# Outputs of 28 heads as float32r products, gains in chunk 0's rows, decays behind the keys, two more chunks of squares on VectorE

## The chip, the core and the metric

The kernel runs on one core of a Trainium2 chip. The core has a matrix engine (TensorE, PE in the profile; its weight loads are PEld), a vector engine (VectorE, DVE), a scalar engine (ScalarE, ACT), GpSimd (POOL), a sync engine that issues most transfers (SyncE, SP), and 16 DMA engines. The engines run their own instruction lists in order and wait for one another by semaphores. The metric is the device time of one execution in microseconds, as the median of several runs.

## The reference

The program is a two-layer decoder trunk on 256 tokens with 16 learned prefix tokens in front (T = 272), width 2048, 16 heads of 128, everything in float32.

```python
h = concat(meta_tokens, x)                       # 272 x 2048
for layer in (0, 1):
    a = rms_norm(h, norm_attn[layer])
    if layer == 0:                               # forgetting attention
        q, k, v, f = split(a @ fox_w_in)
        c = cumsum(log_sigmoid(f + fox_b_f))
        s = q k^T * scale + c[q] - c[k], masked; p = softmax(s); o = p v
        h = h + o @ fox_w_o
    else:                                        # stick-breaking attention, shared K and V
        k, v = split(rms_norm(h, kv_norm) @ w_kv); q = a @ sb_w_q
        z = q k^T * scale
        p = exp(log_sigmoid(z) + later sums of log_sigmoid(-z)), masked; o = p v
        h = h + o @ sb_w_o
    h = h + relu(rms_norm(h, norm_mlp[layer]) @ w_up) ** 2 @ w_down
return rms_norm(h, final_norm)[16:]
```

Queries are handled in blocks: the 16 prefix tokens, then two blocks of 128. A block sees the keys up to its own end.

## The kernel before

Activations lie feature-major: 16 chunks of 128 features on the partitions, tokens along the free axis. `hT` is the residual stream. A weight matrix is streamed in 128x1024 pieces `raw` (two k-chunks of 512 columns) on SP's queue through four buffers.

**Products in three parts.** Large products are not made in float32. A float32 operand is split into a part hi, rounded to float32r, and the remainder lo: ACT copies hi, DVE subtracts lo. For weights these are `whi` and `wlo` (L220, L221), each with a ring of four buffers; for activations the object `Split` holds them (`x_a`, `x_o`, `x_u` and others). `gemm_group` (products at L168) computes four chunks of output, in the accumulators `acc_0` to `acc_3`, over 16 k-chunks in four blocks `kb`, with three float32r products for each pair of k-chunk and output chunk: hi with hi, hi with lo, lo with hi. Small products, in attention and norms, are made in float32 directly; the profile draws such a product as two records (x2).

**Attention.** Heads come in four groups of four. For each group of layer 0 one `gemm_group` makes the queries, one the keys and one the values; layer 1 makes all queries first and then keys and values by group. Scores are put into a tile `s`, one of three buffers with the tag "s". In layer 0 `decays` (L483) first fills `s` with forget-gate differences and mask, from `fk`, which arrives by a transfer. `evac_k` writes the keys `kT` (L337) and their hi and lo parts `kh` and `kl` (L339). The probabilities are turned key-major by 32x32 transposes and copies, `turned` into `pt`, and the values token-major by `token_major` into `vt` (L380). Both are cut into pieces that `PLANS` puts at the `kb` steps of the next `gemm_group`, behind the splits of that step's weights; `turns` makes this table.

`outputs` (L415 to L447) then makes the four heads' outputs: a small product `pc` for corner parts, and for each head one float32 product `po` of 128x256 (L421: the first key block for both query blocks) and one of 128x128 (L424: the second key block for the second query block). DVE adds the corner parts (L426), and `put_split` writes the outputs as hi and lo (L446 on ACT, L447 on DVE) into `x_o`. Outputs of one group run at the end of the next group's query product in layer 0, and before block 3 of its key product in layer 1; those of the last group of each layer run inside the first group of the output projection, `out_proj`.

**Start.** `load_x` loads `hT` in chunks (L261) between the pieces of the first weight (L203), with the six norm gains `g_sb` as a transfer of their own behind chunk 0 (L263). `split_chunk` scales and splits a chunk (ACT L122, DVE L123).

**End.** The final norm needs the sum of squares over the 16 chunks of the last residual. Chunks 0 to 11 are squared on ACT and summed on DVE (`normf.add`, L140). `add_squares` (L676) multiplies this sum, and the squares of chunks 12, 13 and 14 each, with a column of 1/2048 on PE, two products of 128x1 each time; chunk 15 follows at L703. Three products `warm` (L718) follow, then `pr_fin` (L723), which spreads the factor, and the output is scaled on DVE and GpSimd and stored.

**What sets the order.** The kernel is written in a tile framework that orders instructions by a simulated timeline at build time. `tc.issue_after` and `behind` (an order without a semaphore, on PE) fix single places, and `pinned` keeps the products of a `gemm_group` in written order. So the written order is only a part of the actual order, which is shown below where it matters.

Of the kernel before, what the change touches and what calls it, by code (L numbers as in the profile page):

```python
# [34 lines left out]
def yoco_kernel(ctx: ExitStack, tc: tile.TileContext, hT_in, gains, b_f, w_f, w_qkv0, w_o0, w_up, w_dn,  # L35
# [17 lines left out]
    hT = const.tile([P, NC, T], F32, name="hT")  # L53
    g_sb = const.tile([P, 6, NC], F32, name="g_sb")
# [124 lines left out]
    def gemm_group(wblk, sp, t0, evac, before={}, after={}, load_x=None, widen=False, mid={}):  # L179
# [9 lines left out]
        for kb in range(4):  # L189
# [15 lines left out]
            for hf in range(2):  # L205
# [11 lines left out]
                for o, no, c0, c1 in boxes:  # L217
                    src = raws[hf][:, o:o + no, c0:c1]
# [40 lines left out]
    def load_x(chunks):  # L259
        c0, n = chunks[0], len(chunks)  # L260
        nc.sync.dma_start(hT[:, c0:c0 + n, :], hT_in[:, c0:c0 + n, :])  # L261
        if c0 == 0:
            nc.sync.dma_start(g_sb, gains)  # L263
        for c in chunks:
            split_chunk(xa, G_A0, c)
# [65 lines left out]
    def keys(label):  # L331
# [4 lines left out]
        def evac(m, acc):  # L336
            nc.vector.tensor_tensor(out=kT[:, m, :], in0=acc, in1=box["rstd"], op=ALU.mult)  # L337
            nc.scalar.activation(kh[:, m, :], kT[:, m, :], AF.Copy)
            nc.vector.tensor_tensor(out=kl[:, m, :], in0=kT[:, m, :], in1=kh[:, m, :].bitcast(F32), op=ALU.subtract)  # L339
# [11 lines left out]
    def turned(s, label):  # L351
# [13 lines left out]
        return pt.rearrange("p (h k) -> p h k", h=4), piece  # L365
# [6 lines left out]
    def token_major(vT, label):  # L372
# [9 lines left out]
        return vt.rearrange("p h (b t) -> p h b t", t=P), piece  # L382
# [5 lines left out]
    def turns(turn_p, turn_v, p, v):  # L388
# [23 lines left out]
    def outputs(g, ao, p, v, pm_sb, vm_sb, label):  # L412
# [4 lines left out]
        for pr in range(2):  # L417
            po = patt.tile([P, 2, 256], F32, tag="patt", name=f"po_{label}_{pr}")
            for i in range(2):
                j = 2 * pr + i  # L420
                ins = nc.tensor.matmul(po[:, i, :], v[:, j, 0, :], p[:, j, :2 * P], start=i == 0, stop=False)  # L421
                if i == 0:
                    behind(ins)
                nc.tensor.matmul(po[:, i, P:], v[:, j, 1, :], p[:, j, 2 * P:], start=False, stop=i == 1)  # L424
# [26 lines left out]
    for g in range(4):  # L451
# [28 lines left out]
        def decays(j):  # L480

            for i, (o, n) in enumerate(((0, 144), (144, T))):
                nc.vector.scalar_tensor_tensor(out=s[:, j, o:o + n], in0=fk[:, j, :n],  # L483
                                               scalar=fq_sb[:, i, 4 * g + j:4 * g + j + 1],
                                               in1=maskA[:, o:o + n], op0=ALU.subtract, op1=ALU.add)
# [22 lines left out]
        def meta(g=g, qm=qm, kT=kT, s0=s0, fk=fk):  # L508
# [3 lines left out]
            nc.vector.scalar_tensor_tensor(out=s0.rearrange("p (h k) -> p h k", h=4), in0=fk[:, :, :32],  # L512
                                           scalar=fqm_sb[:, g:g + 1], in1=maskM, op0=ALU.subtract, op1=ALU.add)
# [7 lines left out]
        probs, turn_p = turned(s, f"0_{g}")  # L521
# [3 lines left out]
        gemm_group(w_qkv0[3 * g + 2], xa, 0, evac_v, {2: meta}, early(turn_p, plan[0]))  # L525

        vm, vc = packed(vT[:, :, 0:32], f"vm_{g}"), corners(vT[:, :, P:144], vT[:, :, 256:T], f"vc_{g}")
        vals, turn_v = token_major(vT, f"0_{g}")
# [97 lines left out]
    for g in range(4):  # L626
# [22 lines left out]
        probs, turn_p = turned(r, f"1_{g}")  # L649

        vT, evac_v = values(f"1_{g}")
        gemm_group(w_kv[2 * g + 1], xc, 0, evac_v, after=early(turn_p, PLANS[1][0]))

        vc = corners(vT[:, :, P:144], vT[:, :, 256:T], f"vc1_{g}")
        vals, turn_v = token_major(vT, f"1_{g}")
# [8 lines left out]
        turning = turns(turn_p, turn_v, *PLANS[1][1:])  # L664
# [9 lines left out]
    def add_squares(src, first, last):  # L674
        for b in range(2):
            nc.tensor.matmul(pms[:, b:b + 1], src[:, M + b * P:M + (b + 1) * P], mean_w[:, 0:1],  # L676
                             start=first and b == 0, stop=last and b == 1)
# [110 lines left out]
```

## Time and profile before

| | us |
|---|---|
| median of 3 runs | 2270.52 (2270.18 to 2270.52) |
| profiled execution | 2269.09 |
| its span | 2267.4 |
| PE busy | 2257.4 |
| DVE busy | 1372.5 |
| ACT busy | 1115.9 |

The granted TensorE clock in the profile is 0.999 of full speed. A timeline row gives start, busy time, engine, line, operation, out<-in, stationary shape and moving shape for PE, and count; the bracket is idle time before it and what ended it. Successive rows of one engine can overlap, since products are pipelined; the pace of a series is the distance of the starts divided by the count. In a table by groups, the numbers behind the first bar are total and mean (ns), and those behind the second are idle time before the group and its releasers.

### The profile page before, as it was taken

What the parts mean: (1) busy time and instruction counts of PE and PEld (TensorE: products, weight loads), DVE (VectorE), ACT (ScalarE), POOL (GpSimd) and SP (SyncE); (2) the same over time, 40 slices, a digit from 0 to 9 for tenths busy, and PEclk for the clock granted to TensorE, in tenths of its full rate; (3) what the DMA queues carried; (4) which work ended last, traced back from release to release, by engine and by line L of the source; (5) the groups of instructions that cost most, each with busy time, mean ns of one, the idle gap of its engine ahead of it and who ended that gap; (6) DMA issues with size and microseconds to landing.
All of it is one profiled execution on the core that took longest, in us unless ns stands there. A gap on an engine that the chain in (4) does not pass through costs nothing.

```text
span 2267.4 us, 44750 instructions
## 1 busy us (share of the span) xinstructions
PE 2257.4 (100%) x18860; PEld 2252.3 (99%) x18860; DVE 1372.5 (61%) x1967; ACT 1115.9 (49%) x1545; POOL 32.7 (1%) x75
## 2 busy tenths in 40 slices
PE   9999999999999999999999999999999999999998
PEld 9999999999999999999999999999999999999998
DVE  7877676554455455455566688876555555555554
ACT  6554565443354344344444567655544543544554
POOL 0000000000000000000000000000000000000000
PEclk9999999999999999999999999999999999999999
DMA  7545545555555555555555544455655656556563
GB/s 247 177 160 173 182 159 175 181 174 177 186 172 182 177 175 185 173 185 177 171 192 185 179 159 159 163 192 186 201 190 189 203 186 203 189 189 202 186 204 132
DMA packets 115993, 412.31 MB, mean 182 GB/s; under 512 B 13504, under 2 KB 15184, under 8 KB 115792
## 3 DMA queue, kind: packets, MB, share of 16 engines
q1 hardware_dynamic: 113904, 406.29, 55.2%
q8 instruction: 147, 2.41, 0.4%
q10 hardware_dynamic: 1888, 3.17, 0.4%
q14 instruction: 54, 0.44, 0.1%
HBM read 407.29 MB, written 2.11 MB: 181 GB/s over the span
## 4 chain that ended last, share of the span: by engine, by line
PE 99%; DMA 0%; DVE 0%; ACT 0%; SPq 0%; issue 0%; DVEq 0%; ACTq 0%
PE acc L168 97%; PE po L421 1%; PE ps L348 1%; PE ps L346 0%; PE po L424 0%; DMA raw<-w_qkv 0%; DVE ob L730 0%; PE pf L295 0%; PE pc L415 0%; PE ps L510 0%; PE pom L541 0%; PE pvm L535 0%; SPq L261 0%; PE pr_fin L723 0%; PE pms_fin L676 0%; ACT whi L220 0%
## 5 line engine op out<-in xcount | busy, mean ns | idle before, releaser
L221 DVE TENSOR_TENSOR wlo<-raw,whi 128x1024 fp32r<-128x1024 f32 (+1 forms) x773 | 926.9, 1216 | 657.0 <-ACT whi L220 648.7
L220 ACT ACTIVATE whi<-raw 128x1024 fp32r<-128x1024 f32 (+1 forms) x773 | 797.3, 1051 | 934.9 <-PE acc L168 901.7
L168 PE MATMUL acc<-x_u,whi 128*128 128x272 f32 (+1 forms) x4096 | 642.9, 281 | 0.0
L168 PE MATMUL acc<-x_m,whi 128*128 128x272 f32 (+1 forms) x4096 | 642.6, 281 | 0.0
L168 PEld LDWEIGHTS acc<-x_u,whi 128*128 128x128 f32 x4096 | 565.9, 188 | 0.0
L168 PEld LDWEIGHTS acc<-x_m,whi 128*128 128x128 f32 x4096 | 565.7, 188 | 0.0
L168 PE MATMUL acc<-x_u,wlo 128*128 128x272 f32 (+1 forms) x2048 | 440.8, 281 | 0.0
L168 PE MATMUL acc<-x_m,wlo 128*128 128x272 f32 (+1 forms) x2048 | 440.7, 281 | 0.0
L168 PE MATMUL acc<-x_a,whi 128*128 128x272 f32 (+1 forms) x2048 | 353.0, 285 | 0.6 <-ACT whi L220 0.6
L168 PEld LDWEIGHTS acc<-x_u,wlo 128*128 128x128 f32 x2048 | 323.3, 188 | 0.0
L168 PEld LDWEIGHTS acc<-x_m,wlo 128*128 128x128 f32 x2048 | 323.2, 188 | 0.0
L168 PEld LDWEIGHTS acc<-x_a,whi 128*128 128x128 f32 x2048 | 300.0, 188 | 1.8 <-ACT whi L220 1.2
L168 PE MATMUL acc<-x_a,wlo 128*128 128x272 f32 (+1 forms) x1024 | 253.1, 285 | 0.0
L168 PE MATMUL acc<-x_kv,whi 128*128 128x272 f32 x1024 | 192.6, 287 | 0.0
L168 PEld LDWEIGHTS acc<-x_a,wlo 128*128 128x128 f32 x1024 | 175.5, 188 | 0.5 <-issue 0.4
L168 PE MATMUL acc<-x_o,whi 128*128 128x272 f32 (+1 forms) x1024 | 161.5, 282 | 0.0
L168 PEld LDWEIGHTS acc<-x_kv,whi 128*128 128x128 f32 x1024 | 160.1, 188 | 0.0
L168 PE MATMUL acc<-x_kv,wlo 128*128 128x272 f32 x512 | 146.8, 287 | 0.0
L168 PEld LDWEIGHTS acc<-x_o,whi 128*128 128x128 f32 x1024 | 141.7, 188 | 0.0
L252 DVE TENSOR_TENSOR hT<-acc,hT 128x272 f32<-128x272 f32 (+1 forms) x159 | 68.6, 431 | 83.2 <-PE acc L168 83.0
L168 PE MATMUL acc<-x_o,wlo 128*128 128x272 f32 (+1 forms) x512 | 110.3, 282 | 0.0
L168 PEld LDWEIGHTS acc<-x_kv,wlo 128*128 128x128 f32 x512 | 96.4, 188 | 0.0
(192 smaller groups left out, 1063.6 us busy)
## 6 DMA issues: line engine op xcount, KB each, us to landing
raw<-w_up SPq DMA_DIRECT2D x256, 512.0 KB, 3.9
raw<-w_dn SPq DMA_DIRECT2D x256, 512.0 KB, 4.1
raw<-w_qkv SPq DMA_DIRECT2D x92, 512.0 KB, 4.1
raw<-w_o SPq DMA_DIRECT2D x64, 512.0 KB, 4.2
raw<-w_kv SPq DMA_DIRECT2D x64, 512.0 KB, 3.8
raw<-w_q SPq DMA_DIRECT2D x32, 512.0 KB, 4.6
fk<-f_dram ACTq DMA_DIRECT2D x4, 544.0 KB, 5.3
raw<-w_qkv SPq DMA_DIRECT2D x7, 256.0 KB, 4.5
```

Of the source, the lines that this page charges most:

```text
L168: ins = nc.tensor.matmul(*args, **kw).ins
L220: on_act = nc.scalar.activation(hp, src, AF.Copy)
L221: on_dve = nc.vector.tensor_tensor(out=lp, in0=src, in1=hp.bitcast(F32), op=ALU.subtract)
L252: nc.vector.tensor_tensor(out=hT[:, c, t0:], in0=acc, in1=hT[:, c, t0:], op=ALU.add)
L348: nc.tensor.matmul(ps[:, 144:416], qs[a][:, j, :], ks[b][:, j, :], start=i == 0, stop=i == 2)
L421: ins = nc.tensor.matmul(po[:, i, :], v[:, j, 0, :], p[:, j, :2 * P], start=i == 0, stop=False)
```

## The change

Four parts.

1. **Outputs.** For 28 of 32 heads (all of layer 0, groups 0 to 2 of layer 1), the 128x256 product of `po` is made as three float32r products. A new function `divide` in `turned` splits the first 256 columns of each head of `pt` into `ph` and `pl` (tiles with the tag "s"), one in `token_major` splits the first key block of the values into the halves hi and lo of one tile `vs`. `turns` calls each behind the last piece of its plan. The 128x128 product stays float32. Group 3 of layer 1 is not divided.
2. **Start.** The gains are put in front of chunk 0's rows, in the same transfer (`rows`, 128x368). Chunk 0's hi part is computed on DVE instead of ACT. The splits of the first four chunks are called from the weight loop, in order with the weights' splits, and the products of the first k-chunk are ordered by part.
3. **Decays.** For group 0 of layer 0, the eight decays are issued behind the last `kl`, and the prefix tokens' decay behind them.
4. **End.** Chunks 12 and 13 are summed on DVE as well. `add_squares` for the sum and for chunk 14 is called in `last_chunk`, behind the last accumulation. A fourth `warm` product is added.

On PE, this is where group 3 of layer 0 makes its outputs, within the first group of the output projection (`acc` from `x_o`), before:

```order
L168 MATMUL acc_3_3929<-x_o_142,wlo_2_0_4089 128x272
L415 MATMUL pc_3_4126<-pm_sb_3_4003,vm_sb_3923 128x128
L421 MATMUL po_3_0_4129<-pt_3_3649,vt_3_3922 128x256
L424 MATMUL po_3_0_4129<-pt_3_3649,vt_3_3922 128x128
...
L421 MATMUL po_3_1_4137<-pt_3_3649,vt_3_3922 128x256
L424 MATMUL po_3_1_4137<-pt_3_3649,vt_3_3922 128x128
...
L168 MATMUL acc_0_3926<-x_o_142,whi_2_1_4092 128x272 x2
```

and after the change:

```order
L447 MATMUL pc_3_4176<-pm_sb_3_4046,vm_sb_3966 128x128
L172 MATMUL acc_0_3969<-x_o_141,whi_2_1_4139 128x272 x2
...
L172 MATMUL acc_1_3970<-x_o_141,whi_2_1_4139 128x272
L456 MATMUL po_3_0_4179<-ph_3_4073,vs_3_4149 128x256
L456 MATMUL po_3_0_4179<-pl_3_4074,vs_3_4149 128x256
...
L172 MATMUL acc_2_3971<-x_o_141,whi_2_1_4139 128x272
L456 MATMUL po_3_0_4179<-ph_3_4073,vs_3_4149 128x256
L459 MATMUL po_3_0_4179<-pt_3_3692,vt_3_3965 128x128
...
L459 MATMUL po_3_1_4191<-pt_3_3692,vt_3_3965 128x128
L172 MATMUL acc_2_3971<-x_o_141,whi_2_1_4139 128x272
```

Each head's first product has become three, and the scheduler put 7 products of the projection ahead of them and 10 among them, so that 8 are left between the outputs and block 3, where 24 were. In the other six groups the outputs stay in one piece, each head as ph with vs, pl with vs, ph with vs, and the 128x128 product.

On DVE, group 0 of layer 1, ahead of its outputs, before (`vt` is the turned values, `po` and `x_o` belong to the outputs):

```order
L380 STREAM_TRANSPOSE vt_0_15038<-vT_0_14780 32x4x2x32 x7
L221 TENSOR_TENSOR wlo_3_0_15289<-raw_3_0_15284,whi_3_0_15288 128x2x512
L221 TENSOR_TENSOR wlo_3_1_15293<-raw_3_1_15285,whi_3_1_15292 128x2x512
L221 TENSOR_TENSOR wlo_0_0_15422<-raw_0_0_15417,whi_0_0_15421 128x2x512
L221 TENSOR_TENSOR wlo_0_1_15426<-raw_0_1_15418,whi_0_1_15425 128x2x512
L426 TENSOR_TENSOR po_0_0_15268<-po_0_0_15268,pm_sb_0_15118 128x4x16
```

and after:

```order
L402 STREAM_TRANSPOSE vt_0_15096<-vT_0_14838 32x4x2x32 x7
L231 TENSOR_TENSOR wlo_3_0_15362<-raw_3_0_15357,whi_3_0_15361 128x2x512
L384 TENSOR_TENSOR pl_0_15269<-pt_0_14837,ph_0_15268 128x4x256
L410 TENSOR_TENSOR vs_0_15279<-vt_0_15096,vs_0_15279 128x4x128
L231 TENSOR_TENSOR wlo_3_1_15366<-raw_3_1_15358,whi_3_1_15365 128x2x512
L231 TENSOR_TENSOR wlo_0_0_15495<-raw_0_0_15490,whi_0_0_15494 128x2x512
L231 TENSOR_TENSOR wlo_0_1_15499<-raw_0_1_15491,whi_0_1_15498 128x2x512
L461 TENSOR_TENSOR po_0_0_15333<-po_0_0_15333,pm_sb_0_15176 128x4x16
```

Two subtractions now stand between the two weight splits of block 3.

On PE, the end of the program, before (`acc_1` to `acc_3` are the last three chunks' accumulators):

```order
L168 MATMUL acc_0_26155<-x_u_3_24290,wlo_3_1_26348 128x256 x2
L676 MATMUL pms_fin<-mean_w,ssq_fin 128x1 x2
L168 MATMUL acc_1_26156<-x_u_3_24290,whi_3_0_26343 128x256 x2
...
L168 MATMUL acc_3_26158<-x_u_3_24290,whi_3_0_26343 128x256
L676 MATMUL pms_fin<-mean_w,sq_fin_26366 128x1 x2
L168 MATMUL acc_3_26158<-x_u_3_24290,whi_3_0_26343 128x256
...
L168 MATMUL acc_3_26158<-x_u_3_24290,wlo_3_1_26348 128x256 x2
L676 MATMUL pms_fin<-mean_w,sq_fin_26384 128x1 x2
L676 MATMUL pms_fin<-mean_w,sq_fin_26402 128x1 x2
L703 MATMUL pms_fin<-mean_w,sq_fin_26419 128x1 x2
L718 MATMUL warm<-mean_w 128x128 x3
```

and after:

```order
L172 MATMUL acc_0_26258<-x_u_3_24393,wlo_3_1_26451 128x256 x2
L172 MATMUL acc_1_26259<-x_u_3_24393,whi_3_0_26446 128x256 x2
...
L172 MATMUL acc_3_26261<-x_u_3_24393,wlo_3_1_26451 128x256 x2
L717 MATMUL pms_fin<-mean_w,ssq_fin 128x1 x2
L717 MATMUL pms_fin<-mean_w,sq_fin_26501 128x1 x2
L745 MATMUL pms_fin<-mean_w,sq_fin_26520 128x1 x2
L760 MATMUL warm<-mean_w 128x128 x4
```

Four pairs of squares ahead of the last chunk's have become two, and none stands among the accumulations.

The diff, without what only renames:

```diff
@@ split_chunk
-        nc.scalar.activation(sp.hi[:, c], hT[:, c, sp.t0:], AF.Copy, scale=g)
+        if sp is xa and c == 0:
+            nc.vector.tensor_scalar(sp.hi[:, c], hT[:, c, sp.t0:], g, None, op0=ALU.mult)
+        else:
+            nc.scalar.activation(sp.hi[:, c], hT[:, c, sp.t0:], AF.Copy, scale=g)
@@ gemm_group
                 for o, no, c0, c1 in boxes:
+                    if load_x is not None and kb == c0 == 0:
+                        if hf == o == 0:
+                            split_chunk(xa, G_A0, 0)
+                        else:
+                            with tc.issue_after(on_act.ins), tc.issue_after(on_dve.ins):
+                                split_chunk(xa, G_A0, 2 * hf + o)
...
-                if t0:
+                if load_x is not None:
+                    pinned[0] = kb == part == 0
+                if t0 or pinned[0] and load_x is not None:
@@ load_x
-        nc.sync.dma_start(hT[:, c0:c0 + n, :], hT_in[:, c0:c0 + n, :])
-        if c0 == 0:
-            nc.sync.dma_start(g_sb, gains)
+        first, end = (6 * NC + c * T if c else 0 for c in (c0, c0 + n))
+        nc.sync.dma_start(rows[:, first:end], hT_in[:, first:end])
         for c in chunks:
-            split_chunk(xa, G_A0, c)
+            if c >= 4:
+                split_chunk(xa, G_A0, c)
@@ turned
+        probs = [pt]
+
+        def divide():
+            hi, lo = (att.tile([P, 4, 416], F32R, tag="s", bufs=3, name=f"p{t}_{label}")[:, :, :2 * P] for t in ("h", "l"))
+            nc.scalar.activation(hi, pt[:, :, :2 * P], AF.Copy)
+            nc.vector.tensor_tensor(out=lo, in0=pt[:, :, :2 * P], in1=hi.bitcast(F32), op=ALU.subtract)
+            probs.extend((hi, lo))
@@ token_major
+        vals = [out]
+
+        def divide():
+            vs = att.tile([P, 4, T], F32R, tag="kv", name=f"vs_{label}")
+            hi, lo = (vs[:, :, t:t + P] for t in (0, P))
+            nc.scalar.activation(hi, out[:, :, 0, :], AF.Copy)
+            nc.vector.tensor_tensor(out=lo, in0=out[:, :, 0, :], in1=hi.bitcast(F32), op=ALU.subtract)
+            vals.extend((hi, lo))
@@ turns
-            if kb in p:
-                turn_p(*p[kb])
-            if kb in v:
-                turn_v(*v[kb])
+            for (turn, divide), plan in ((turn_p, p), (turn_v, v)):
+                if kb in plan:
+                    turn(*plan[kb])
+                if divided and kb == max(plan):
+                    divide()
@@ outputs
-                ins = nc.tensor.matmul(po[:, i, :], v[:, j, 0, :], p[:, j, :2 * P], start=i == 0, stop=False)
-                if i == 0:
-                    behind(ins)
-                nc.tensor.matmul(po[:, i, P:], v[:, j, 1, :], p[:, j, 2 * P:], start=False, stop=i == 1)
+                wide = [(v[1][:, j], p[1][:, j]), (v[1][:, j], p[2][:, j]), (v[2][:, j], p[1][:, j])] if len(v) == 3 else [
+                    (v[0][:, j, 0, :], p[0][:, j, :2 * P])]
+                for k, (vk, pk) in enumerate(wide):
+                    ins = nc.tensor.matmul(po[:, i, :], vk, pk, start=i == k == 0, stop=False)
+                    if i == k == 0:
+                        behind(ins)
+                nc.tensor.matmul(po[:, i, P:], v[0][:, j, 1, :], p[0][:, j, 2 * P:], start=False, stop=i == 1)
@@ layer 0, keys of a group
-        gemm_group(w_qkv0[3 * g + 1], xa, 0, evac_k, after={j: (lambda j=j: decays(j)) for j in range(4)})
+        gemm_group(w_qkv0[3 * g + 1], xa, 0, evac_k,
+                   after={j: (lambda j=j: decays(j)) for j in range(4)} if g else {})
+        if g == 0:
+            for j in range(4):
+                with tc.issue_after(box["kl"].ins):
+                    decays(j)
@@ layer 1
-        turning = turns(turn_p, turn_v, *PLANS[1][1:])
+        turning = turns(turn_p, turn_v, *PLANS[1][1:], divided=g < 3)
@@ the end
-        if c < NC - 4:
+        if c < NC - 2:
             normf.add(c)
         else:
-            if c == NC - 4:
-                add_squares(normf.acc, True, False)
...
-            add_squares(sq, False, c == NC - 1)
...
+        add_squares(normf.acc, True)
+        add_squares(box["sq"], False)
...
-    for _ in range(3):
+    for _ in range(4):
         behind(nc.tensor.matmul(warm[:, :P], mean_w, mean_w, start=True, stop=True))
```

More of the change, by code (lines that the diff above doesn't have):

```diff
@@ L34, in yoco_kernel @@
 @with_exitstack
[L35 removed]
+def yoco_kernel(ctx: ExitStack, tc: tile.TileContext, hT_in, b_f, w_f, w_qkv0, w_o0, w_up, w_dn,
                 w_kv, w_q1, w_o1, outT):
@@ L672, in yoco_kernel, with add_squares @@
     box = {}
[L674 removed]
+    def add_squares(src, first):
         for b in range(2):
[L676 to L677 removed]
+            ins = nc.tensor.matmul(pms[:, b:b + 1], src[:, M + b * P:M + (b + 1) * P], mean_w[:, 0:1],
+                                   start=first and b == 0, stop=False)
+            behind(ins)
+            queued[:] = [ins.ins]
     normf = Norm("fin", M)
     def last_evac(c):
[L682 removed]
+        if c < NC - 2:
             normf.add(c)
         else:
[L685 to L687 removed]
+            sq = box["sq"] = tmp.tile([P, T], F32, tag="sq", name=f"sq_fin_{c}")
             nc.scalar.activation(sq[:, M:], hT[:, c, M:], AF.Square)
[L689 removed]
         nc.scalar.activation(hT[:, c, M:], hT[:, c, M:], AF.Copy, scale=g_sb[:, G_FIN, c:c + 1])
```

45 lines of the change are left out of this document (24 added, 21 removed).

## The prediction

> **What bounds the kernel now.** I read the page's busy row and the chain that ended last first, then the timeline of TensorE (PE) at its two visible idle places.
>
> ```profile
> PE 2257.4 (100%) x18860; PEld 2252.3 (99%) x18860; DVE 1372.5 (61%) x1967; ACT 1115.9 (49%) x1545; POOL 32.7 (1%) x75
> PE 99%; DMA 0%; DVE 0%; ACT 0%; SPq 0%; issue 0%; DVEq 0%; ACTq 0%
> ...
> 7.22 1.26 PE L168 MATMUL acc<-x_a,whi 128*128 128x272 f32 x8 [0.56 <-ACT whi L220]
> 2258.34 0.82 PE L723 MATMUL pr_fin<-ident,fin 128*128 128x128 f32 x5 [0.40 <-DVE fin L714]
> ```
>
> PE is busy for the whole span, and the chain is PE for 99%. Between its first product and the last transposes I find two stalls: 0.56 us at the start, for a split weight block, and 0.40 us at the end, for the last norm. So a step is worth something only if it takes work from PE, starts PE earlier, or makes PE wait where it does not wait now. VectorE (DVE, 61%) and ScalarE (ACT, 49%) have room on average; what matters is their lead over PE at each place.
>
> **Outputs, 28 heads.** A float32 product is drawn as two records (x2).
>
> ```profile
> 108.57 0.60 PE L421 MATMUL po<-pt,vt 128*128 128x256 f32 x2
> 109.00 0.38 PE L424 MATMUL po<-pt,vt 128*128 128x128 f32 x2
> 109.22 0.60 PE L421 MATMUL po<-pt,vt 128*128 128x256 f32 x2
> ...
> 110.53 0.60 PE L421 MATMUL po<-pt,vt 128*128 128x256 f32 x2
> ...
> 2243.71 1.98 PE L168 MATMUL acc<-x_u,whi 128*128 128x256 f32 x16
> 2245.52 1.07 PE L168 MATMUL acc<-x_u,wlo 128*128 128x256 f32 x8
> ```
>
> Heads begin 0.653 us apart (108.57 to 110.53, three heads): 0.43 to 0.44 for the 256-wide product, 0.22 for the 128-wide one, by the starts of the first three rows. The 256-wide one becomes three float32r products of the same width. A float32r product of 256 columns has a pace of 0.113 us (2243.71 to 2245.52 over 16). The 128-wide one stays float32, and now stands alone among float32r work. The nearest such case is this:
>
> ```profile
> 325.34 0.29 PE L168 MATMUL acc<-x_o,whi 128*128 128x272 f32 x1
> 325.47 0.38 PE L541 MATMUL pom<-pm_sb,vm_sb 128*128 128x128 f32 x2
> 325.61 0.37 PE L168 MATMUL acc<-x_o,whi 128*128 128x272 f32 x1
> ```
>
> The float32r product behind it is drawn 0.37 long instead of 0.29, so the excursion costs its 0.14 of starts and about 0.08 more: 0.22 to 0.23, what it costs now. Per head: 3 x 0.113 + 0.23 = 0.57, against 0.653, saves 0.08; 28 heads save 2.3. Float32r just behind float32 work can run slower: in the tail rows below, 8 products take 0.94 (2252.37 to 2253.31), a pace of 0.1175, and with it a head saves 0.07, 28 heads 2.0. Here float32 work is always one product away, so I take the slower pace: **-2.0**. Ends: 0 if every return to float32r loses another 0.07, which no row shows, and -2.6 at the fast pace with 0.22 for the excursion.
>
> The Trainium skill (FP8 and Floating Point Precision, section TensorE Precision Notes) says that true float32 makes four passes through the array. By this rule a float32r product is a quarter of the float32 one, 0.109, and the saving is a quarter for each head, 0.109, or 3.0 us in all; the rows' ratio is 3.8.
> Three products also need three loads of the stationary operand instead of one.
>
> ```profile
> L168 PEld LDWEIGHTS acc<-x_u,whi 128*128 128x128 f32 x4096 | 565.9, 188 | 0.0
> ```
>
> A load is drawn 0.188 long. The first row of the page counts as many loads as products (x18860 of both), and the pace of 0.113 holds with a load for each product, so loads lie beside products. Rival (d) is that here they don't. The Trainium skill speaks against the change here (TensorE: Matmul & The Clock Gate, section LDWEIGHTS (loading the stationary operand)): its formula gives an estimate of 107 ns for a load of 128 columns; were none of that hidden, a head would take about 0.89 and 28 heads 6.6 us more. This trace shows it hidden.
>
> **The divides that feed them.** Per group: one ACT copy and one DVE subtraction of 128x1024, and one each of 128x512. Nearest forms:
>
> ```profile
> L220 ACT ACTIVATE whi<-raw 128x1024 fp32r<-128x1024 f32 x764 | 792.1, 1056 | 932.6 <-PE acc L168 901.7 <-issue 14.7 <-ACT sq_m L139 6.4
> L446 ACT ACTIVATE x_o<-po 128x512 fp32r<-128x512 f32 x16 | 9.6, 598 | 16.2 <-DVE po L426 15.3
> ...
> L221 DVE TENSOR_TENSOR wlo<-raw,whi 128x1024 fp32r<-128x1024 f32 x764 | 921.3, 1223 | 653.6 <-ACT whi L220 645.3
> L447 DVE TENSOR_TENSOR x_o<-po,x_o 128x512 fp32r<-128x512 f32 x16 | 11.1, 692 | 1.6 <-ACT x_o L446 1.3
> ```
>
> ACT gets 1.06 + 0.60 = 1.65 us, DVE 1.22 + 0.69 = 1.92, for each of seven groups. They stand between weight splits, so the question is the lead of the splits behind them. The last block before the outputs (its wlo made, then first used):
>
> ```profile
> 97.22 1.23 DVE L221 TENSOR_TENSOR wlo<-raw,whi 128x1024 fp32r<-128x1024 f32 x1 [0.78 <-ACT whi L220]
> 103.41 0.29 PE L168 MATMUL acc<-x_a,wlo 128*128 128x272 f32 x1
> ...
> 1321.47 2.36 DVE L221 TENSOR_TENSOR wlo<-raw,whi 128x1024 fp32r<-128x1024 f32 x2
> 1326.87 0.60 PE L421 MATMUL po<-pt,vt 128*128 128x256 f32 x2
> 1330.49 0.28 PE L168 MATMUL acc<-x_kv,wlo 128*128 128x272 f32 x1
> ...
> 72.00:111.00 39.00, 39.00 (x314) 38.80 (x313) 32.38 (x66) 24.64 (x41) 4.25 (x6) 1.00 0.60 193
> ```
>
> In layer 0 it is made at 98.45 and used at 103.41: 5.0 us of lead. In layer 1, 1323.83 and 1330.49: 6.7. Both exceed 1.92, and also the 3.57 that ACT and DVE would take one after the other. The window row (length, PE, loads, DVE, ACT) says that DVE is busy 32.4 of 39 us in the densest of these stages: 6.6 idle, of which a divide takes 1.9. In layer 1 the operands are ready in time too: the DVE subtractions go between the two splits of the row at 1321.47, so they end near 1322.7 + 1.9 = 1324.6, and the outputs start at 1326.87. The cover is this lead; **0**. Ends: 0 and, in the rival below, a stall for each group.
>
> The divides take slots of two rings. Hi and lo of the probabilities are now the fourth and fifth tenants of three "s" buffers, so the next group's decays wait for the outputs' last float32 product. They are written in layer 0 before the next scores only, and DVE has idle time there; 0, within the same rival.
>
> **Group 3 of layer 0.** Its outputs lie inside the first output projection. The order moves 7 and 10 projection products ahead of and among them, and leaves 8 (about 1.0 us) behind, where 24 were.
>
> ```profile
> 333.95 1.44 DVE L447 TENSOR_TENSOR x_o<-po,x_o 128x512 fp32r<-128x512 f32 x2
> 336.56 0.41 PE L168 MATMUL acc<-x_o,whi 128*128 128x272 f32 x2
> ```
>
> Now the outputs' lo is finished at 335.39, 1.17 before the block that reads it. With 16 products fewer behind the outputs (2.0 us) the cover would be gone, but the two pairs of heads are finished apart, and the second pair is read only six products into the block (0.74). What is left is 0 to 0.2: **+0.1**.
>
> **The tail.** Squares of chunks 12 and 13 are added on DVE, and all pairs on PE go behind the last accumulation.
>
> ```profile
> L140 DVE TENSOR_TENSOR ssq_fin<-ssq_fin,sq_fin 128x256 f32<-128x256 f32 x11 | 4.7, 424 | 3.9 <-ACT sq_fin L139 3.9
> ...
> 2250.51 0.50 PE L676 MATMUL pms_fin<-mean_w,ssq_fin 128*128 128x1 f32 x4
> 2252.37 1.10 PE L168 MATMUL acc<-x_u,whi 128*128 128x256 f32 x8
> 2253.31 0.63 PE L168 MATMUL acc<-x_u,wlo 128*128 128x256 f32 x4
> 2253.90 0.50 PE L676 MATMUL pms_fin<-mean_w,sq_fin 128*128 128x1 f32 x4
> 2255.62 0.95 PE L676 MATMUL pms_fin<-mean_w,sq_fin 128*128 128x1 f32 x8
> 2256.56 0.60 PE L703 MATMUL pms_fin<-mean_w,sq_fin 128*128 128x1 f32 x4
> ```
>
> From 2250.51 to 2255.62, 5.11 us, PE does two pairs of squares and the last 36 products. Without the pairs, 36 x 0.113 = 4.08 at the fast pace: **-1.0**; at 0.1175, -0.9. Behind the last accumulation stand eight records, as now (chunks 13 and 14; then the sum and chunk 14), so nothing is late next. The two DVE additions cost 0.42 each, between accumulations 1.4 us apart. The fourth warming product fills a part of the 0.40 that PE waits there anyway: 0, at worst +0.1.
>
> **The start.** The gains come in chunk 0's rows: one issue less on SP.
>
> ```profile
> 1.25 0.42 SPq L263 DMA_DIRECT2D g_sb<-gains  x1
> 2.19 0.43 SPq L203 DMA_DIRECT2D raw<-w_qkv  x1
> 6.53 0.63 ACT L220 ACTIVATE whi<-raw 128x512 fp32r<-128x512 f32 x1 [0.33 <-DMA raw<-w_qkv]
> 17.43 1.21 DVE L221 TENSOR_TENSOR wlo<-raw,whi 128x1024 fp32r<-128x1024 f32 x1
> 18.70 0.39 PE L168 MATMUL acc<-x_a,wlo 128*128 128x272 f32 x1
> ```
>
> Two issues take 0.94 (1.25 to 2.19), so every later one can go 0.47 earlier, among them the block whose landing at 6.53 ends PE's first stall. Chunk 0's hi moves from ACT to the then idle DVE, which starts PE's first products earlier but not that block. The ends are -0.47, if it lands as much earlier, and 0, if bandwidth sets the landing, or if the split that is used at 18.70, ready at 18.64, then stalls PE. Nothing decides between them: **-0.25**.
>
> **Group 0's decays.**
>
> ```profile
> 59.11 2.86 DVE L483 SCALAR_TENSOR_TENSOR s<-fk,fq_sb,maskA 128x144 f32<-128x144 f32 x8 [2.19 <-DMA fk<-f_dram]
> ```
>
> DVE waits here 2.19 us for a transfer, with the fourth key and the lo parts of the keys queued behind it. Afterwards these and the weight splits go first, and the eight decays, 2.86 us, stand right ahead of the scores' reductions. PE has no stall here now, so there is nothing to gain: **0**.
>
> **The sum.** -2.0 - 1.0 - 0.25 + 0.1 = -3.15. The profiled execution took 2269.09 (span 2267.4 and 1.69 around it), which is 1.43 below the median of 2270.52; it would become 2265.9, and the median 2267.3.
>
> **Rivals.** (a) Slower: the divides stall PE. They are issued ahead of the weight splits of their block, and the rings of four splits pass a delay on. If the lead that counts were not 5 to 6.7 us but the 2.3 by which layer 1's divided operands precede the outputs (1324.6 to 1326.87), the 3.57 us in series would stall PE 1.3 a group, 8.9 for seven, and the median would be 2276. From 0.46 a group (3.2 / 7) the gain is gone, from 1.1 ((2275.06 - 2267.3) / 7) the kernel is measurably slower. The rows above speak against it; the dense window, where less than 5 us of DVE would stay idle, for it. With a stall in two or three groups only, 2269 to 2271.
>
> (b) More: float32r at the four-pass ratio (-3.0), the whole of the start (-0.47) and of the tail (-1.1): 2266.0, at the border of what counts as faster. For it is only that the fast pace is the commoner one.
>
> (c) Less: switching between float32 and float32r costs 0.07 more on each return, so the outputs give nothing, and only tail and start remain: 2269.3. For it is the slower pace behind float32; against it the excursion at 325.47.
>
> (d) Weight loads that don't lie beside the products: 3 x (0.113 + 0.188) + 0.23 = 1.13 a head, 0.48 more than now, 13.4 in all, so 2270.5 + 13.4 - 1.2 = 2282.7. The pace of 0.113 nearly excludes it.
>
> **How the numbers follow.** 0.2% of the median is 4.54 us, about what a measurement of this kernel can tell from no change: faster is below 2265.98, slower above 2275.06. My forecast has 0.70, (b) 0.08, (c) 0.12, (a) 0.09 with a third of it as a few small stalls, (d) 0.01. (b) falls on both sides of the bound. So faster 0.05, same 0.88, slower 0.07. The forecast alone runs from 2265.9 to 2268.4; with (c) and the small stalls above, and (b) below, the range is 2265.4 to 2269.9.
>
> **What would show it.** Right: the heads' output products start about 0.57 apart; no idle time of PE at 103 to 111, 1326 to 1331 and 331 to 337 of the old count; the stall near 6.7 us is longer but ends some tenths earlier; from the last accumulations' start the 36 products run at 0.113 without a record of squares between them. Wrong: idle time of PE with a weight split or a divide as its releaser, which is (a); heads 0.65 apart, which is (c); a new stall between 8 and 20 us, which takes the start's term back.

## The result and the profile after

The changed kernel takes 2266.39 us (median of 18 runs, 2265.59 to 2267.34), the kernel before 2270.14 (18 runs beside it, 2269.19 to 2271.64). The ratio is 0.9983, with a 95% interval of 0.9976 to 0.9990: 3.75 us or 0.17% less, clear of zero, and inside the 0.2% that the prediction called no measurable change. The profiled execution took 2266.31, with a span of 2264.6; that of before 2269.09 and 2267.4. The two profiles therefore differ by 2.8, the medians by 3.75. What the profiles don't show is taken up below.

The page of the changed kernel, busy row and chain:

```profile
PE 2254.6 (100%) x18882; PEld 2251.1 (99%) x18882; DVE 1385.6 (61%) x1984; ACT 1125.9 (50%) x1558; POOL 29.2 (1%) x75
...
PE 99%; DMA 0%; DVE 0%; ACT 0%; DVEq 0%; issue 0%
```

PE has 2.8 us less to do, and DVE 13 and ACT 10 more. The chain is still PE. The table of waits of PE (us in total, times, longest) lists all that is left:

```profile
PE idle L65 <- DVE eps L733: 1.1, 1, 1.1
PE acc L172 <- ACT whi L230: 0.7, 1, 0.7
PE pr_fin L765 <- DVE fin L756: 0.2, 1, 0.2
```

No divide and no later weight split stands there. The timeline of PE at the first outputs, `pc`, then the heads, then the next products of weights:

```profile
108.55 0.38 PE L447 MATMUL pc<-pm_sb,vm_sb 128*128 128x128 f32 x2
108.68 0.36 PE L456 MATMUL po<-ph,vs 128*128 128x256 f32 x1
108.89 0.28 PE L456 MATMUL po<-pl,vs 128*128 128x256 f32 x1
109.00 0.28 PE L456 MATMUL po<-ph,vs 128*128 128x256 f32 x1
109.12 0.38 PE L459 MATMUL po<-pt,vt 128*128 128x128 f32 x2
109.26 0.36 PE L456 MATMUL po<-ph,vs 128*128 128x256 f32 x1
...
110.42 0.36 PE L456 MATMUL po<-ph,vs 128*128 128x256 f32 x1
...
111.00 0.50 PE L172 MATMUL acc<-x_a,whi 128*128 128x272 f32 x2
```

A head takes 0.58 (108.68 to 110.42, three heads). These rows are rounded to hundredths. In the mean over the 20 heads of this trace that follow directly on another head, the distances of starts are 0.204 for the first float32r product, which comes behind a float32 one, 0.118 for each of the next two, and 0.139 for the float32 one: 0.578 in all.

The same number follows from a finer reading. PE makes the same 18,432 products of weights in both kernels; taking the k-th of each trace, its start after the change less its start before is the time gained up to there (negative where it is earlier). Over the outputs of a group this difference falls by 0.30 to 0.31 six times. Over those of group 3 of layer 0 it falls by 0.30, and then rises by 0.10. Over the end it falls by 1.03. At the start it rises by 0.2. In sum: -6 x 0.305 - 0.20 - 1.03 + 0.2 = -2.86, and the last product is 2.83 earlier.

The end, on PE:

```profile
2248.71 1.07 PE L172 MATMUL acc<-x_u,whi 128*128 128x256 f32 x8
...
2252.33 0.62 PE L172 MATMUL acc<-x_u,wlo 128*128 128x256 f32 x4
2252.79 0.50 PE L717 MATMUL pms_fin<-mean_w,ssq_fin 128*128 128x1 f32 x4
2253.15 0.58 PE L717 MATMUL pms_fin<-mean_w,sq_fin 128*128 128x1 f32 x4
2253.67 0.60 PE L745 MATMUL pms_fin<-mean_w,sq_fin 128*128 128x1 f32 x4
```

The last 36 products take 4.08 (2248.71 to 2252.79), and the squares follow without a wait.

The start, on PE, ACT and SP (a row of `SPq` is the issue of transfers):

```profile
4.98 0.50 PE L172 MATMUL acc<-x_a,whi 128*128 128x272 f32 x2
6.22 1.01 PE L172 MATMUL acc<-x_a,whi 128*128 128x272 f32 x6 [0.74 <-ACT whi L230]
7.07 0.66 PE L172 MATMUL acc<-x_a,wlo 128*128 128x272 f32 x4
7.56 1.15 PE L172 MATMUL acc<-x_a,whi 128*128 128x272 f32 x8
...
5.75 0.42 ACT L230 ACTIVATE whi<-raw 128x256 fp32r<-128x256 f32 x1 [0.91 <-DMA raw<-w_qkv]
6.49 0.62 ACT L230 ACTIVATE whi<-raw 128x512 fp32r<-128x512 f32 x1
...
0.81 0.86 SPq L274 DMA_DIRECT2D rows<-hT_in  x2
1.72 0.42 SPq L207 DMA_DIRECT2D raw<-w_qkv  x1
```

The second weight chunk is issued 0.47 earlier, at 1.72. But now the second half of the first chunk, on ACT's queue, comes late (ACT waits 0.91 for it until 5.75), and PE stalls after two products, where it had made all twelve of that chunk before it stalled. The second chunk's products begin at 7.56 instead of 7.22. The prediction's sign of the start, a longer stall near 6.7 that ends some tenths earlier, did not appear in this profile.

### The profile page after: what moved, and what is told of

Its sections match the earlier page's. It is cut to its first block, busy times and chain, and to the rows that moved or that the text cites. A ratio compares the mean times of both kernels' runs of the same rounds, so it can differ in the third digit from the quotient of the medians.

```text
span 2264.6 us, 44834 instructions
## 1 busy us (share of the span) xinstructions
PE 2254.6 (100%) x18882; PEld 2251.1 (99%) x18882; DVE 1385.6 (61%) x1984; ACT 1125.9 (50%) x1558; POOL 29.2 (1%) x75
## 4 chain that ended last, share of the span: by engine, by line
PE 99%; DMA 0%; DVE 0%; ACT 0%; DVEq 0%; issue 0%
PE acc L172 97%; PE ps L361 1%; PE po L456 1%; PE ps L359 0%; PE po L459 0%; DMA raw<-w_qkv 0%; DVE ob L772 0%; PE pf L307 0%; PE pc L447 0%; PE pom L582 0%; PE ps L550 0%; PE pvm L576 0%; PE pr_fin L765 0%; PE pf_sum L312 0%; ACT sq_fin L744 0%; ACT rows L746 0%
## 5 line engine op out<-in xcount | busy, mean ns | idle before, releaser
L264 DVE TENSOR_TENSOR rows<-acc,rows 128x272 f32<-128x272 f32 (+1 forms) x159 | 68.6, 432 | 81.0 <-PE acc L172 80.7
```

The costliest lines, as they stand in the source:

```text
L264: nc.vector.tensor_tensor(out=hT[:, c, t0:], in0=acc, in1=hT[:, c, t0:], op=ALU.add)
```

## The experiments

Medians are compared with the kernel before in the same series, since single runs of one kernel lie up to 2.9 us apart (the kernel before, 2269.16 to 2272.03). The experiments ran in four series, each on another chip. "In the trace" means the difference of starts, product for product, against the profile of before. One part alone moves the time by less than its interval of about 0.09% each way (2 us), so what is said of one part rests on its trace, or on several runs that agree.

| run | median, us | before, us | difference | ratio, 95% interval |
|---|---|---|---|---|
| e1_outputs | 2268.26 | 2269.97 | -1.71 | 0.9993 (0.9984 to 1.0002) |
| e2_end | 2268.52 | 2269.97 | -1.45 | 0.9994 (0.9985 to 1.0003) |
| e3_start | 2268.97 | 2269.97 | -1.00 | 0.9996 (0.9988 to 1.0005) |
| e5_no_start | 2267.12 | 2269.97 | -2.85 | 0.9989 (0.9980 to 0.9997) |
| e6_merged | 2269.08 | 2270.01 | -0.93 | 0.9996 (0.9987 to 1.0005) |
| e7_order | 2270.21 | 2270.01 | +0.20 | 1.0001 (0.9993 to 1.0010) |
| e8_two_gains | 2270.90 | 2270.01 | +0.89 | 1.0004 (0.9995 to 1.0013) |
| e9_all32 | 2267.93 | 2270.01 | -2.08 | 0.9990 (0.9981 to 0.9999) |
| e10_twice | 2268.48 | 2270.28 | -1.80 | 0.9992 (0.9983 to 1.0001) |
| e11_two_chunks | 2265.84 | 2270.28 | -4.44 | 0.9981 (0.9972 to 0.9990) |
| after_again | 2266.18 | 2270.28 | -4.10 | 0.9982 (0.9973 to 0.9991) |
| e12_merged_start | 2266.05 | 2270.08 | -4.03 | 0.9983 (0.9974 to 0.9992) |

### The outputs alone

The edit: of the diff above, only the parts in `turned`, `token_major`, `turns` and `outputs`, and what calls them.

> The kernel before with the divided outputs alone. The forecast's term: 28 heads x 0.07 to 0.08 us = 2.0 to 2.3 us less than before, and in the trace output heads about 0.58 apart and no idle time of PE ahead of a weight split. Rival (divides stall PE): less than 1 us gained or a loss, with idle time of PE released by a weight split. Rival (outputs are worth what the whole change gained, 3.75 us by the medians, less the end's 1.0): 2.7 us.

In the trace the difference at the start is +0.15 and at the last product -1.86: the outputs give 2.01. The median gives 1.71, which differs from it by less than its uncertainty. PE waits for no divide and for no weight split behind the first ones. One wait is new, 0.3 us at the very end (from 2254.71 to 2254.99, for the square of the last chunk); it comes behind the last product of weights, so the 2.01 doesn't hold it. The forecast's term stands, and by the trace both rivals fall: the outputs neither stall nor carry the surplus.

### The end alone

The edit: only `add_squares`, `last_evac`, `last_chunk` and the fourth warming product.

> The kernel before with the change at the end alone (two more chunks summed on VectorE, all pairs of squares behind the last accumulation, a fourth warming product). Forecast's term: 1.0 us less (0.9 to 1.1); from the start of the last 36 products to the first pair of squares 4.08 us. Rival: the sums wait for the two added VectorE additions, and the gain is given back as idle time of PE before the squares: 0 to 0.5.

In the trace the difference is +0.13 from the start on, falls to -0.90 over the last 36 products, and stays: the end gives 1.03. The table of waits has no wait of a product of squares. The median shows 1.45, which the trace doesn't explain; this run, too, has the start of before, whose executions differ.

### The start alone, and all but the start

The edit of the first: only the parts in `split_chunk`, `load_x`, the weight loop of `gemm_group`, and the joined input array. The second is the changed kernel without these.

> The kernel before with the change at the start alone (gains in chunk 0's rows, chunk 0's hi on VectorE). Three theories: the forecast's, 0.25 us less (0 to 0.47); that the one profile of the changed kernel is typical, in which the products lag 0.2 us behind those of before from the first weight block on: 0.2 us more; that the start carries what the medians show beyond outputs and end (3.75 - 2.2 - 1.0): 0.5 to 0.6 us less.

> The changed kernel with the start as before: outputs, end and decays alone. Forecast: 2.9 us less than before (2.0 + 1.0 - 0.1). If the start loses 0.2 us, it is faster than the changed kernel, 3.9 to 4.0 less than before; if the start gives 0.5 to 0.6, 3.1 to 3.2 less.

By the medians the start gives 1.0 alone, and 0.9 (3.75 - 2.85) to 1.25 (4.10 - 2.85) within the whole: more than forecast, and not the loss of the one profile. The traces say less. After the start has passed (480 products), the four profiles with the start of before stand at 0, +0.15, +0.13 and +0.98 (before, e1, e2, e5), those with the gains merged at +0.20 and -0.11 (changed kernel, e3) so far. The +0.98 shows how the start of before can go wrong. The timeline of the run of all but the start, on PE and ACT:

```profile
18.41 1.26 PE L168 MATMUL acc<-x_a,whi 128*128 128x272 f32 x8 [0.40 <-ACT whi L220]
...
17.30 1.06 ACT L220 ACTIVATE whi<-raw 128x1024 fp32r<-128x1024 f32 x1 [1.18 <-DMA raw<-w_qkv]
```

In the profile of before the same split, on ACT:

```profile
16.29 1.06 ACT L220 ACTIVATE whi<-raw 128x1024 fp32r<-128x1024 f32 x1 [0.51 <-DMA raw<-w_qkv]
```

The third block's first weights land so that their split begins at 17.30 instead of 16.29, and PE waits a second time. This is the split whose remainder had 0.05 us to spare at 18.70 in the prediction's rows. So the profile of before was a lucky one in this place; it was also faster (2269.09) than every other run of its series (lowest 2269.19).

### Which part of the start

The first has the gains in chunk 0's rows and nothing else. The second has the rest of the start. The third is the kernel before with one line more:

```diff
             nc.sync.dma_start(g_sb, gains)
+            nc.sync.dma_start(const.tile([P, 6, NC], F32, name="g_2"), gains)
```

> The kernel before with the gains in chunk 0's rows alone; chunk 0's hi stays on ScalarE and the products keep their order. The start alone measured 1.0 us less than before, in medians. If the missing transfer issue does it (0.47 us for each transfer behind it, and the stalls that follow from late weight blocks): 0.7 to 1.0 less. If the moved hi part and the order of the first products do it: 0 to 0.2 less.

> The counterpart: gains in a transfer of their own as before, but chunk 0's hi on VectorE, the first four splits called with the weights' splits, the first products ordered by part. If the missing issue carries the start's gain: 0 to 0.2 less than before, or a little more; if the order carries it: 0.7 to 1.0 less.

> The kernel before with the gains' transfer issued twice, the second time to a tile that nothing reads. If one small transfer in this queue costs its issue slot all the way (landing of the second weight chunk, and of those behind): 0.5 to 1.0 us more than before. If it costs nothing because bandwidth sets the landings: 0 to 0.2 more.

By the medians one small transfer less gives 0.93, one more costs 0.89, and the new order gives nothing (+0.20). No interval excludes zero. But all eleven runs with the merged transfer lie below the median of before in their series, and all eleven with two transfers above it; those with the order alone lie on both sides, four below and seven above. With the difference of 1.0 above, sign and size agree. In the traces after 480 products: -0.31 (merged), +0.44 (order), +0.69 (two). The restart of PE in the merged run, the one with two transfers, and their first products, in this order:

```profile
4.98 1.25 PE L169 MATMUL acc<-x_a,whi 128*128 128x272 f32 x4
...
7.17 1.15 PE L169 MATMUL acc<-x_a,whi 128*128 128x272 f32 x8
```

```profile
4.99 1.49 PE L168 MATMUL acc<-x_a,whi 128*128 128x272 f32 x5
...
7.80 1.26 PE L168 MATMUL acc<-x_a,whi 128*128 128x272 f32 x8 [0.22 <-ACT whi L220]
```

The second weight chunk begins at 7.17 without a listed wait, and at 7.80 with a second small transfer, against 7.22 before. So one more transfer shows in the trace where the prediction looked for it (0.58 later), one less hardly does (0.05 earlier). That the start's gain is the missing transfer's, not the order's, rests on the medians.

> The changed kernel whose start has the merged transfer alone: chunk 0's hi is back on ScalarE, the first four splits and the first products are in the order of before. The merged transfer alone gave -0.9 us and the order alone +0.2 beside before; if the two add up here too, this is the same as the changed kernel or up to 0.3 us faster (3.8 to 4.3 less than before). If the order is needed once outputs and end are changed: 0.2 or more slower than the changed kernel.

This run undoes the order in the changed kernel and keeps the merged transfer:

```diff
-        if sp is xa and c == 0:
-            nc.vector.tensor_scalar(sp.hi[:, c], hT[:, c, sp.t0:], g, None, op0=ALU.mult)
-        else:
-            nc.scalar.activation(sp.hi[:, c], hT[:, c, sp.t0:], AF.Copy, scale=g)
+        nc.scalar.activation(sp.hi[:, c], hT[:, c, sp.t0:], AF.Copy, scale=g)
...
-                if t0 or pinned[0] and load_x is not None:
+                if t0:
```

It is as fast as the changed kernel (-4.03; -3.75 and -4.10). The order of the first products and the moved hi part do nothing that these medians can tell.

### One transfer less again, and the changed kernel again

The first run takes chunk 1 into the first transfer as well, so that one issue less stands ahead of the second weight chunk. The second run is the changed kernel as it is.

```diff
-        first, end = (6 * NC + c * T if c else 0 for c in (c0, c0 + n))
-        nc.sync.dma_start(rows[:, first:end], hT_in[:, first:end])
+        first, end = (6 * NC + c * T if c else 0 for c in (c0, max(c0 + n, 2)))
+        if c0 != 1:
+            nc.sync.dma_start(rows[:, first:end], hT_in[:, first:end])
```

> The changed kernel with chunks 0 and 1 (and the gains) in one transfer of 128x640, one issue less again ahead of the second weight chunk. By the last pairs (merged -0.9, doubled +0.9 us for one issue): 0.5 to 0.9 less than the changed kernel. Rival: what counts is when bytes land; the first transfer is larger, chunk 0 comes later, and the gain is 0 or a loss of up to 0.5.

> The changed kernel itself, for the comparison on one chip and for a second profile of its start: 3.75 us less than before; the products of the start not 0.2 later than in the profile of before, as in the first profile, but by the mean of the four profiles with merged gains about 0.1 earlier (within -0.3 to +0.2).

The changed kernel repeats (-4.10). Its start stands at +0.31 after 480 products, which misses what was expected of it (0.1 earlier, at most +0.2 late): the profiles of its start vary too, over all eight with merged gains from -0.31 to +0.31. With two chunks in the first transfer the median is 0.34 lower, the lowest of all kernels here, and less than the 0.5 to 0.9 expected; three of its eleven runs lie at 2267.5 to 2267.7, above every run of the changed kernel beside it (highest 2266.55). Its first products come later, as the rival said (5.51 instead of 4.98 in the first profile of the changed kernel), and it gains behind them: +0.59 after 120 products, -0.18 after 480. Whether it is better than the changed kernel isn't settled.

### The cover of the divides

Each divide is made twice, with the same values. The eight warming products at the end are float32r, 128 columns wide, in place of four float32 ones.

```diff
             nc.scalar.activation(hi, pt[:, :, :2 * P], AF.Copy)
             nc.vector.tensor_tensor(out=lo, in0=pt[:, :, :2 * P], in1=hi.bitcast(F32), op=ALU.subtract)
+            nc.scalar.activation(hi, pt[:, :, :2 * P], AF.Copy)
+            nc.vector.tensor_tensor(out=lo, in0=pt[:, :, :2 * P], in1=hi.bitcast(F32), op=ALU.subtract)
...
-    for _ in range(4):
-        behind(nc.tensor.matmul(warm[:, :P], mean_w, mean_w, start=True, stop=True))
+    for _ in range(8):
+        behind(nc.tensor.matmul(warm[:, :P], mean_r, mean_r, start=True, stop=True))
```

> The changed kernel with each divide made twice (the second result overwrites the first with the same values): 3.57 us more for each of seven groups, 7.1 in all. If the lead of the weight splits, 5.0 and 6.7 us, is what hides the divides: DVE's part, 3.8, still fits, so at most small stalls in layer 0 where ACT and DVE work in turn: 0 to 1 us more than the changed kernel. If the divides are just hidden and the cover is nearly used up (rival a): 7 x 1.3 to 7 x 3.6 = 9 to 25 us more. The warming products at the end are eight float32r ones of 128 columns instead of four float32 ones, which shows the pace of a narrow float32r product; they stand ahead of a wait and should cost nothing.

It is 2.3 us slower than the changed kernel (-1.80 against -4.10). In the trace it loses 1.9 of that at one place, group 3 of layer 0, and at most 0.03 in each of the other six groups, each of which took 3.57 us more of ACT and DVE work. The wait table and the timeline of PE at the one place:

```profile
PE acc L172 <- DVE x_o L486: 0.5, 1, 0.5
PE po L460 <- DVE vs L414: 0.3, 1, 0.3
...
334.62 0.39 PE L460 MATMUL po<-ph,vs 128*128 128x256 f32 x1 [0.34 <-DVE vs L414]
337.64 0.39 PE L172 MATMUL acc<-x_o,whi 128*128 128x272 f32 x1 [0.49 <-DVE x_o L486]
```

So a divide made twice over stays hidden in six groups, as forecast, and rival (a) is excluded for them. In layer 1 that is not by the lead of the weight splits alone. In its group 0 the second subtraction of the values ends at 1328.41, after the outputs have begun (1327.88), and ten products of the key group stand among the outputs there (1328.20 to 1329.57), where the changed kernel has none. The seventh group has no room: what stalls there isn't a weight split, but the outputs waiting for their own operands, and the projection waiting for the outputs.

### The last group divided as well

```diff
-        turning = turns(turn_p, turn_v, *PLANS[1][1:], divided=g < 3)
+        turning = turns(turn_p, turn_v, *PLANS[1][1:])
```

> The changed kernel with group 3 of layer 1 divided too, so that all 32 heads are made in float32r. By the term of the other seven groups (0.31 us a group in the traces, 0.21 where the outputs lie inside the output projection) 0.2 to 0.3 less than the changed kernel, 4.0 less than before. Rival: the divides stall the output projection of layer 1, which follows at once: the same as the changed kernel or slower, with idle time of PE near the outputs.

It is slower than the changed kernel: -2.08 against -3.75 to -4.10. The rival was right. In the trace it loses 1.8 over these outputs, instead of gaining 0.3. The timeline of PE:

```profile
1482.11 1.07 PE L172 MATMUL acc<-x_o,wlo 128*128 128x256 f32 x8
1483.02 0.29 PE L456 MATMUL po<-ph,vs 128*128 128x256 f32 x1
...
1484.64 0.38 PE L459 MATMUL po<-pt,vt 128*128 128x128 f32 x2
1485.96 1.83 PE L172 MATMUL acc<-x_o,whi 128*128 128x256 f32 x8 [0.94 <-ACT x_o L481]
```

Products of the projection that lay behind the outputs have been moved ahead of them, while the divided operands were awaited, and none is left behind them: the next block needs these very outputs, and PE stands until ACT and DVE have split them. It is the same mechanism that the prediction priced at group 3 of layer 0, where eight products are left; here all of the cover is gone.

## Why the prediction was right, point by point

The forecast was 2267.3 (2265.4 to 2269.9), 3.2 below the median that was known (the sum of -3.15 gives 2267.37). The measured median is 2266.39, which is 3.75 below that of before beside it. That is nearer to rival (b)'s 2266.0 than to the forecast, but not by that rival's mechanism: the outputs gave 2.1 and not 3.0, the end 1.03, and only a larger start is borne out, by medians. Of the other rivals none came true.

- **Outputs: -2.0 forecast, -2.1 measured** in the trace (seven groups of 0.30 to 0.31; with group 3's loss of 0.1 it is the 2.0 of e1). A head takes 0.578, forecast 0.58. The parts are those of the forecast too: all three float32r products run at the slower pace (0.118, forecast 0.1175), and the first one takes 0.086 on top, which with the 0.139 of the float32 product makes 0.225 for the excursion, forecast 0.23. By the four-pass rule of the Trainium skill (FP8 and Floating Point Precision, section TensorE Precision Notes) the saving was estimated at 3.0; the trace shows 2.1. Weight loads are hidden (18,882 loads beside as many products, and a head of 0.578 instead of 1.13), so rival (d) fell.
- **Divides: 0 forecast, 0 measured.** The seven DVE subtractions of each kind are what the nearest forms said:

```profile
L384 DVE TENSOR_TENSOR pl<-pt,ph 128x1024 fp32r<-128x1024 f32 x7 | 8.6, 1222 | 0.1
L410 DVE TENSOR_TENSOR vs<-vt,vs 128x512 fp32r<-128x512 f32 x7 | 4.8, 685 | 0.0
...
1322.84 0.68 DVE L410 TENSOR_TENSOR vs<-vt,vs 128x512 fp32r<-128x512 f32 x1
1325.88 0.37 PE L456 MATMUL po<-ph,vs 128*128 128x256 f32 x1
```

  Layer 1's operands were ready at 1323.5 for outputs at 1325.88: 2.4 us ahead, forecast 2.3. Made twice, the divides still cost next to nothing in six groups.
- **Group 3 of layer 0: +0.1 forecast, +0.10 measured.** The trace has 7 products of the projection ahead of the outputs, 9 among them (not 10) and 8 behind them. The outputs' split ended at 336.34. In the block that reads it, the starts behind the two rows of PE below slipped by 0.07 and 0.03. No wait is listed for them, so that the split caused them is read from their place alone:

```profile
334.89 1.45 DVE L482 TENSOR_TENSOR x_o<-po,x_o 128x512 fp32r<-128x512 f32 x2
335.55 0.47 PE L172 MATMUL acc<-x_o,whi 128*128 128x272 f32 x2
336.36 0.44 PE L172 MATMUL acc<-x_o,whi 128*128 128x272 f32 x2
```

- **The end: -1.0 forecast, -1.03 measured** in the traces of e2 and of the changed kernel: the last 36 products run at 0.113 without a record of squares among them.
- **Group 0's decays: 0 forecast.** They were not run alone. In the trace of the changed kernel the difference is +0.22 after 120 products, and +0.20 after 480 and up to the first outputs at 108, with the decays between: nothing gained or lost.
- **The start: -0.25 forecast**, and this is the term that was mis-sized, if the medians are followed: -0.9 to -1.25 (e3, e6, and the changed kernel against e5). The step that failed is the way from the issue to the products. The issue of the second weight chunk did go 0.47 earlier, but its products did not start earlier. After 12 products, where they start, the four profiles with the start of before (before, e1, e2, e5) stand at +0.13 in the mean, and the seven with the gains merged into chunk 0's rows alone (after, e3, e6, e9, e10, after_again, e12) at +0.20. After 480 products the means are +0.32 and +0.07. That their difference is the forecast's -0.25 is luck: nearly all of it comes from the one stall of e5 at 18.41, and without e5 the first mean is +0.09. The end of its range, "-0.47, if it lands as much earlier", took the later stalls of the start as they were in one profile. That one issue less saves stalls like that of e5 would fit the medians, but isn't shown.
- **What stays open.** Timed runs of the six kernels whose gains come separately lie 0.1 to 1.1 us above their own profiled execution in the median (mean 0.6), those of the eight with merged gains -0.2 to +0.5 (mean 0.1). The differences stand in the core's spans as well (medians -1.0 for e3, -0.9 for e6, +0.8 for e8), so the time lies between the first and the last instruction; no profile shows what an execution without a profile waits for. Nor do executions differ at the start alone: the pace of some stretches does too, as the last section shows.
- **The sum.** The terms of the traces, -2.0 - 1.0 + 0.2, give the 2.8 between the two profiles; the 0.9 more in the medians is put down to the start by medians alone.

## What to carry to other kernels

When one engine is busy all the time, cost a change as that engine's work, product by product, and ask of everything added elsewhere only how early its result is: here 3.6 us of added work cost nothing in six of seven places, where the splits were 5 to 6.7 us ahead, and 0.1 in the seventh. Where a group's outputs are needed at once, count the work left behind them before moving anything ahead; the same division that gained 0.3 us elsewhere lost 1.8 in group 3 of layer 1. And a start that waits for transfers differs from execution to execution, so it shouldn't be sized from one profile.

## What the runs showed of the hardware

- A float32r product of 128 columns is here no faster than one of 256. The warming products of the run with doubled divides, eight of 128 columns, at the end of the program:

```profile
2256.21 1.09 PE L764 MATMUL warm<-mean_r 128*128 128x128 f32 x8
```

  Eight take 1.09 with the last one's own length of 0.28, so 0.116 from start to start, against 0.113 at 256 columns (2248.71 to 2252.79 above). So three float32r products in place of the float32 product of 128 columns (0.14 of starts and the 0.09 behind it) would have cost 0.35, as an estimate from these rows.
- Some stretches of 256-column products run at 0.118 in one execution and at 0.113 in another, by the same instructions (the changed kernel did both in its two profiles). One such stretch lies between the small product `pvc` and the outputs of group 3 of layer 1. From before, and then from the second profile of the changed kernel (sixteen products, then the start of the next):

```profile
1475.68 2.05 PE L168 MATMUL acc<-x_o,whi 128*128 128x256 f32 x16
1477.56 1.10 PE L168 MATMUL acc<-x_o,wlo 128*128 128x256 f32 x8
...
1473.88 1.98 PE L172 MATMUL acc<-x_o,whi 128*128 128x256 f32 x16
1475.69 1.07 PE L172 MATMUL acc<-x_o,wlo 128*128 128x256 f32 x8
```

  Sixteen take 1.88 in the first and 1.81 in the second. Five runs (e3, e6, e8, e11, after_again) have the faster pace there and gain 0.3 us by it. In e8 alone another stretch, from 1569 to 1582, is slow and loses 0.47. No wait is listed at either place, and what sets the pace wasn't tried.
- One small transfer among the first of SP's queue is worth about 0.9 us by the medians, taken away (e6) or added (e8), where its issue slot is 0.47. One more taken away (e11) gave 0.34, which isn't settled.
